# Attention scores of a hybrid retention and attention block: 288 contraction rows in two full passes and four products of 32 rows

## The chip, the cores and the metric

The kernel runs on one core of a Trainium2 chip. The metric is the device time of one execution, in microseconds (us), taken as the median of repeated runs. TensorE multiplies a stationary operand (loaded by a weight load of its own, the row "PEld") with a moving one of up to 512 columns and writes to PSUM; VectorE (DVE), ScalarE (ACT) and GpSimd (POOL) do the rest; the queue of SyncE (SP) issues most DMAs.

## What is computed

One encoder layer on 1024 tokens of width 1024: a norm, one input projection, eight heads of retention, eight heads of latent attention, one output projection with a gate. The change touches the attention scores alone. Each head has 64 columns of its own (nope) and 32 columns that carry the rotary phase (rope); the rope part of the key is one for all heads:

```python
def attend(blk):
    qn, qr = blk
    s = (jnp.einsum('bqhd,bkhd->bhqk', qn, k_nope)
         + jnp.einsum('bqhd,bkd->bhqk', qr, k_rope))
    p = jax.nn.softmax(s.astype(f32) * sm_scale, axis=-1).astype(v.dtype)
    return jnp.einsum('bhqk,bkhd->bqhd', p, v)
```

## The kernel before, in words

Every product of two f32 matrices is made of three products of a shorter type: each operand is split into a high part and the rest (low), and `mm3` (L64 to L67) adds high x high (L65), low x high (L66) and high x low (L67) into one PSUM bank. ACT writes the high part, DVE or POOL subtracts to get the low one.

After the input projection, the retention (L330 to L446, with 128-row products at L424 and products of 128 or 64 rows at L425) and the latent projections, the loop at L595 makes q and k of all heads with tokens on the partitions: `q4` and `k4` hold 96 columns per head, and L629 copies the rope columns of the key (`krp`) into each head's k. `prep` (L641) prepares one head: for each half of the tokens, four transposes (L652) put the 96 columns of q or k on the partitions, ACT writes the high part (L654, with a scale) and DVE the low part (L655); `vsplit` (L659) splits v. The first head's prep runs before the loop, with two early score blocks (`early_scores`, L670) among the value projections (L692 to L700).

The attention loop (L801) goes over 8 heads of 8 query tiles of 128 queries and, two steps behind (SKEW), over their probabilities. One step does: `scores` for tile n (L713), which is two `mm3` of 96 rows into one of two score tiles `sp` of two PSUM banks each, a maximum on DVE (L720), a scalar step (L721), the exponential on ACT (L723) and a normalisation on POOL (L724, L725); `turn` for tile n-2 (L730), which is eight transposes (L739) through three `pt` banks, casts on ACT (L741) and subtractions on DVE (L742); for every second tile `values` (L744), 24 products of 256 columns into the one `po` bank; and at set tiles (PREP_AT, for head 0 PREP_0) one part of the next head's prep. Head 7 prepares the output projection instead: pages of w_out (`w3page`, L786, in three buffers `w3h`, `w3l`) and splits of the first heads' results (`usplit`, L779). The output projection (L850) follows, one page at a time.

The instructions of each engine run in the order that the planner of the framework gives them from a model of their costs, under the data dependencies; memory that a tile gives back is waited for through semaphores.

## Time and profile before

| | us |
|---|---|
| median of 3 runs | 1059.13 (1057.57 to 1059.34) |
| the profiled execution | 1057.49 |
| its span in the trace | 1055.3 |
| TensorE busy in the span | 1018.1 (96%) |
| VectorE | 581.4 (55%) |
| ScalarE | 426.0 (40%) |
| GpSimd | 404.1 (38%) |

The profile shows one execution. Busy times of TensorE are sums over products that overlap in their pipeline, so the start of one product to the start of the next says more than the length of one. The attention loop fills the span from about 698 to 957 us.

### The profile page before, as it was taken

To read this page: it belongs to the slowest core of one execution; us is meant where nothing else is said; L and a number is where in the kernel's file an instruction comes from. 1 tells how busy PE (TensorE), PEld (TensorE's weight loads), DVE (VectorE), ACT (ScalarE), POOL (GpSimd) and SP (SyncE) were. 2 spreads that over 40 slices of the span, in tenths; PEclk is the share of its full clock that TensorE was granted. 3 is DMA by queue.
4 is the path that set the end of the run, shared out by engine and by line. 5 is a ranking of instruction groups with operands and counts; after the bars stand their busy time and mean duration, and the time that the engine had idled before them with its cause. 6 is when DMAs were issued, how large, how long until landed. Compare 5 with 4: busy or idle time off the path is not lost.

```text
span 1055.3 us, 15223 instructions
## 1 busy us (share of the span) xinstructions
PE 1018.1 (96%) x5736; PEld 888.3 (84%) x5736; DVE 581.4 (55%) x1390; ACT 426.0 (40%) x800; POOL 404.1 (38%) x311
## 2 busy tenths in 40 slices
PE   5899999999999999999999999989999999989998
PEld 4687887888888888998888889879889999878887
DVE  7996546444643534336302116777877777883342
ACT  6654213312321322124322006577767776772100
POOL 2233315213411411224633217943466555873210
PEclk8899999999999999999999999999999999998999
DMA  9721103101110212224654520100000000003522
GB/s 365 264 64 57 41 1 120 41 2 62 63 36 20 85 47 73 102 84 136 201 171 153 183 85 11 41 1 2 20 21 21 2 20 22 21 20 120 169 101 70
DMA packets 30744, 82.27 MB, mean 78 GB/s; under 512 B 3536, under 2 KB 4560, under 8 KB 30672
## 3 DMA queue, kind: packets, MB, share of 16 engines
q1 hardware_dynamic: 25920, 72.92, 20.4%
q10 hardware_dynamic: 4752, 8.39, 2.2%
q8 instruction: 45, 0.74, 0.3%
q14 instruction: 27, 0.22, 0.1%
HBM read 64.52 MB, written 16.78 MB: 77 GB/s over the span
## 4 chain that ended last, share of the span: by engine, by line
PE 82%; DVE 11%; DMA 2%; ACT 2%; issue 2%; POOL 2%; ACTq 0%; DVEq 0%; POOLq 0%
PE acc L65 13%; PE acc L66 13%; PE acc L67 13%; PE pt L739 4%; PE sp L65 4%; PE sp L66 4%; PE sp L67 4%; PE po L66 3%; PE po L67 3%; PE po L65 3%; DVE x L178 2%; DMA wa<-w_ada 2%; PE sm L425 2%; PE sm L424 1%; PE sm L65 1%
## 5 line engine op out<-in xcount | busy, mean ns | idle before, releaser
L81 POOL TENSOR_TENSOR wl<-wr,wh 128x1024 fp32r<-128x1024 f32 (+2 forms) x51 | 115.2, 2268 | 173.2 <-ACT wh L80 148.9
L65 PE MATMUL acc<-wh,hh 128*128 128x512 f32 (+2 forms) x352 | 130.8, 372 | 1.7 <-ACT hh L189 1.7
L66 PE MATMUL acc<-wl,hh 128*128 128x512 f32 (+2 forms) x352 | 130.3, 370 | 0.0
L67 PE MATMUL acc<-wh,hl 128*128 128x512 f32 (+2 forms) x352 | 126.4, 368 | 2.1 <-DVE hl L190 2.1
L725 POOL TENSOR_SCALAR pr<-pr,st 128x1024 f32<-128x1024 f32 x62 | 72.0, 1165 | 101.1 <-DVE st L724 75.5
L65 PE MATMUL acc<-hh,wh 128*128 128x512 f32 x256 | 101.0, 395 | 1.7 <-ACT v L345 1.7
L742 DVE TENSOR_TENSOR pl<-pt,ph 128x512 fp32r<-128x512 f32 x128 | 85.3, 683 | 31.2 <-ACT ph L741 31.1
L66 PE MATMUL acc<-hl,wh 128*128 128x512 f32 x256 | 100.9, 394 | 0.0
L67 PE MATMUL acc<-hh,wl 128*128 128x512 f32 x256 | 100.6, 393 | 0.0
L80 ACT CAST wh<-wr 128x1024 fp32r<-128x1024 f32 (+2 forms) x55 | 53.8, 982 | 104.1 <-PE sm L66 45.1
L741 ACT CAST ph<-pt 128x512 fp32r<-128x512 f32 x128 | 73.1, 591 | 26.6 <-PE pt L739 24.6
L720 DVE TENSOR_REDUCE st<-sp 128x1 f32<-128x1024 f32 x62 | 75.4, 1216 | 6.5 <-PE sp L67 6.4
L66 PE MATMUL po<-pl,vh 128*128 128x256 f32 x256 | 76.5, 299 | 2.1 <-DVE pl L742 2.0
L723 ACT ACTIVATE pr<-sp,st 128x1024 f32<-128x1024 f32 x62 | 69.5, 1121 | 20.8 <-DVE st L721 20.5
L65 PEld LDWEIGHTS acc<-wh,hh 128*128 128x128 f32 x352 | 67.2, 191 | 10.9 <-ACT hh L189 2.1
L67 PEld LDWEIGHTS acc<-wh,hl 128*128 128x128 f32 x352 | 66.0, 188 | 11.1 <-DVE hl L190 3.0
L66 PEld LDWEIGHTS acc<-wl,hh 128*128 128x128 f32 x352 | 67.3, 191 | 8.7
L739 PE MATMUL pt<-ident,pr 128*128 128x128 f32 x496 | 70.2, 274 | 4.0 <-DVE st L724 2.7
L65 PE MATMUL po<-ph,vh 128*128 128x256 f32 x256 | 73.3, 286 | 0.0
L67 PE MATMUL po<-ph,vl 128*128 128x256 f32 x256 | 72.8, 284 | 0.0
L360 POOL TENSOR_TENSOR rb<-t,t 128x128 f32<-128x128 f32 x32 | 14.8, 464 | 135.0 <-PE sm L370 73.4
L739 PEld LDWEIGHTS pt<-ident,pr 128*128 128x128 f32 x496 | 57.9, 141 | 8.5 <-issue 2.9
(353 smaller groups left out, 2474.2 us busy)
## 6 DMA issues: line engine op xcount, KB each, us to landing
x<-w_ada SPq DMA_DIRECT2D x16, 512.0 KB, 7.1
wr<-w_ret SPq DMA_DIRECT2D x16, 512.0 KB, 3.5
wr<-w_rg SPq DMA_DIRECT2D x8, 512.0 KB, 3.5
retD<-ro SPq DMA_DIRECT2D x16, 256.0 KB, 2.1
wr<-w_mg SPq DMA_DIRECT2D x8, 512.0 KB, 3.5
wa<-w_ada SPq DMA_DIRECT2D x8, 512.0 KB, 3.5
wr<-w_out SPq DMA_DIRECT2D x8, 512.0 KB, 4.5
wro<-retD SPq DMA_DIRECT2D x8, 512.0 KB, 3.9
```

What stands on the lines that cost most here:

```text
L65: T.matmul(out, lh, rh, start=first, stop=False, **kw)
L66: T.matmul(out, lh, rl, start=False, stop=False, **kw)
L67: T.matmul(out, ll, rh, start=False, stop=last, **kw)
L80: A.copy(out=hi, in_=raw)
L81: eng.tensor_tensor(out=lo, in0=raw, in1=hi, op=ALU.subtract)
L178: V.scalar_tensor_tensor(out=wa, in0=wa, scalar=1.0, in1=sc, op0=ALU.mult, op1=ALU.mult, accum_out=mp[:, i:i + 1])
L720: V.tensor_reduce(out=st_[:, 0:1], in_=sp, op=ALU.max, axis=AX.X)
L723: A.activation(pr, sp, AF.Exp, bias=st_[:, 1:2], scale=sc_, accum_out=st_[:, 2:3])
L725: G.tensor_scalar(out=pr, in0=pr, scalar1=st_[:, 3:4], scalar2=0.0, op0=ALU.mult, op1=ALU.add)
L739: T.transpose(tp[:, ts_(q)], pr[:, ts_(half * 4 + q)], ident)
L741: A.copy(out=ph[half][:, :, c_], in_=tv)
L742: V.tensor_tensor(out=pl[half][:, :, c_], in0=tv, in1=ph[half][:, :, c_], op=ALU.subtract)
```

## The change

The 288 rows of a score (three products of 96) are laid out anew. A first full product of 128 rows takes q1 (high nope, high rope, low rope) with k1 (high nope, high rope, high rope), a second one q2 (high nope, low nope) with k2 (low nope, high nope). What is left, high rope of q with low rope of k, has 32 rows. Two query tiles are handled together: the eight full products of both come first, then four products of 32 rows, one for each query tile and half of the keys, each on its own 32 partitions and into its own PSUM bank. `issue_after` puts the four behind the last full one on TensorE.

The rows get to their partitions by DMAs on SP's queue (`move`): seven for a half of q, one for a half of k, and 14 once for the rope part of the key. k's tile holds 64 columns per head, so its transposes have 64, and the eight copies of L629 go; `kr` keeps the rope columns. To fit in memory, the low part of q is a buffer of one half (`lo`), `sqh` has one buffer in place of two, w_out pages have two in place of three, and a page is prepared after the products that read its buffer.

```diff
@@ -589,7 +589,9 @@
     vall = p_v.tile([P, H, S], F32, name="vall", tag="vall")
     sqa = p_v.tile([P, S], F32, name="sqa", tag="sqa")
     q4 = [p_qk.tile([P, 4, H, 96], F32, name=f"q4{i}", tag=f"q4{i}") for i in range(2)]
-    k4 = [p_qk.tile([P, 4, H, 96], F32, name=f"k4{i}", tag=f"k4{i}") for i in range(2)]
+    k4 = [p_qk.tile([P, 4, H, 64], F32, name=f"k4{i}", tag=f"k4{i}") for i in range(2)]
+    kr = p_qk.tile([P, NT, 2, 16], F32, name="kr", tag="kr")
+    G.tensor_copy(out=kr, in_=krp)
     qs = [q4[t // 4][:, t % 4] for t in range(NT)]
     ks = [k4[t // 4][:, t % 4] for t in range(NT)]
     for t in range(NT):
@@ -612,7 +614,7 @@
             wh, wl = wkv[j][0]
             mm3(ps, ckh[j][:, ts_(t)], ckl[j][:, ts_(t)], wh[:, 0, 0:512], wl[:, 0, 0:512], j == 0, j == 1)
         pk = ps.rearrange("p (h d) -> p h d", h=8)
-        A.copy(out=ks[t][:, :, 0:64], in_=pk)
+        A.copy(out=ks[t], in_=pk)
         sq = p_ring.tile([P, H, 64], F32, name="sq3", tag="wr", bufs=2)
         A.activation(sq, pk, AF.Square, scale=0.125)
         V.tensor_reduce(out=ss[:, 8:16], in_=sq, op=ALU.add, axis=AX.X)
@@ -622,11 +624,10 @@
         G.tensor_tensor(out=rr, in0=ss, in1=neghalf, op=ALU.pow)
         if t == NT - 1:
             A.activation(ctile("warm", 1), rr[:, 0:1], AF.Exp, scale=0.0)
-        for x_, r0, n in ((qs[t][:, :, 0:64], 0, 64), (qs[t][:, :, 64:96], 16, 32), (ks[t][:, :, 0:64], 8, 64)):
+        for x_, r0, n in ((qs[t][:, :, 0:64], 0, 64), (qs[t][:, :, 64:96], 16, 32), (ks[t], 8, 64)):
             V.tensor_tensor(out=x_, in0=x_, in1=rr[:, r0:r0 + 8].unsqueeze(2).broadcast_to([P, 8, n]), op=ALU.mult)
         qr = qs[t][:, :, 64:96].rearrange("p h (a d) -> p h a d", a=2)
         mla_rope(qr, qr, mtab["Cq"][:, t], mtab["Sq"][:, t], 8, p_uw)
-        A.copy(out=ks[t][:, :, 64:96], in_=krp[:, t].rearrange("p a d -> p (a d)").unsqueeze(1).broadcast_to([P, 8, 32]))
     s_uw.close()
     s_cq.close()
 
@@ -635,8 +636,33 @@
     p_hd = s_hd.enter_context(tc.tile_pool(name="hd", bufs=2, side="left", reuse_waits="tile"))
     sc_ = 96.0 ** -0.5
 
-    def hd_pair(nm):
-        return (p_hd.tile([P, S], F32R, name=nm + "h", tag=nm + "h"), p_hd.tile([P, S], F32R, name=nm + "l", tag=nm + "l"))
+
+
+    k1s = [p_hd.tile([P, S], F32R, name=f"k1{z}", tag=f"k1{z}", bufs=1) for z in range(2)]
+    q3 = p_hd.tile([P, S], F32R, name="q3", tag="q3", bufs=1)
+    k3 = p_hd.tile([P, S], F32R, name="k3", tag="k3", bufs=1)
+
+    def hd_tile(nm):
+        return p_hd.tile([P, S], F32R, name=nm, tag=nm)
+
+    def q_pair():
+        return hd_tile("q1"), hd_tile("q2")
+
+    def move(dst, src):
+        SY.dma_start(out=dst.bitcast(F32), in_=src.bitcast(F32))
+
+    for half in range(2):
+        sl = slice(half * 512, half * 512 + 512)
+        tp = sm()
+        for q in range(4):
+            T.transpose(tp[0:32, ts_(q)], kr[:, half * 4 + q].rearrange("p a d -> p (a d)"), ident)
+        A.copy(out=k1s[1][0:32, sl], in_=tp[0:32])
+        V.tensor_tensor(out=k3[0:32, sl], in0=tp[0:32], in1=k1s[1][0:32, sl], op=ALU.subtract)
+        for z in range(2):
+            for r in (64, 96):
+                move(k1s[z][r:r + 32, sl], k1s[1][0:32, sl])
+        for r in (32, 64, 96):
+            move(k3[r:r + 32, sl], k3[0:32, sl])
 
     def prep(h, bank):
 
@@ -645,15 +671,29 @@
         def tr(nm, src, col, half):
             def go():
                 if half == 0:
-                    ops[nm] = hd_pair(nm)
-                hi, lo = ops[nm]
+                    ops[nm] = (k1s[h % 2], hd_tile("k2")) if nm == "k" else q_pair()
+                x1, x2 = ops[nm]
+                n = 64 if nm == "k" else 96
                 tp = bank()
                 for q in range(4):
-                    T.transpose(tp[0:96, ts_(q)], src[half * 4 + q][:, h], ident)
+                    T.transpose(tp[0:n, ts_(q)], src[half * 4 + q][:, h], ident)
                 sl = slice(half * 512, half * 512 + 512)
-                A.activation(hi[0:96, sl], tp[0:96], AF.Copy, scale=qk96[0:96, col:col + 1])
-                V.scalar_tensor_tensor(out=lo[0:96, sl], in0=tp[0:96], scalar=qk96[0:96, col:col + 1],
-                                       in1=hi[0:96, sl], op0=ALU.mult, op1=ALU.subtract)
+                A.activation(x1[0:n, sl], tp[0:n], AF.Copy, scale=qk96[0:n, col:col + 1])
+                lo = x2[:, sl] if nm == "k" else p_hd.tile([P, 512], F32R, name="lo", tag="lo", bufs=1)
+                V.scalar_tensor_tensor(out=lo[0:n], in0=tp[0:n], scalar=qk96[0:n, col:col + 1],
+                                       in1=x1[0:n, sl], op0=ALU.mult, op1=ALU.subtract)
+                if nm == "k":
+                    move(x2[64:128, sl], x1[0:64, sl])
+                else:
+                    move(x1[96:128, sl], lo[64:96])
+                    move(x2[0:64, sl], x1[0:64, sl])
+                    move(x2[64:128, sl], lo[0:64])
+                    for e in range(2):
+                        src_ = x1[64:96, sl].rearrange("p (b e n) -> p b e n", e=2, n=P)[:, :, e]
+                        c0 = 512 * (h % 2) + 256 * half
+                        for z in range(2):
+                            g = 64 * e + 32 * z
+                            move(q3[g:g + 32, c0:c0 + 256].rearrange("p (b n) -> p b n", n=P), src_)
             return go
 
         def vsplit():
@@ -664,19 +704,30 @@
             ops["v"] = (vh, vl)
         return ops, [tr("k", ks, 1, 0), tr("k", ks, 1, 1), tr("q", qs, 0, 0), tr("q", qs, 0, 1), vsplit]
 
+    def score_blocks(ops, h, blocks):
+
+        (q1, q2), (k1, k2) = ops["q"], ops["k"]
+        for i, banks in blocks:
+            for half, ps in enumerate(banks):
+                sl = slice(half * 512, half * 512 + 512)
+                T.matmul(ps, q1[:, ts_(i)], k1[:, sl], start=True, stop=False)
+                full = T.matmul(ps, q2[:, ts_(i)], k2[:, sl], start=False, stop=False)
+        with tc.issue_after(full.ins):
+            for i, banks in blocks:
+                for half, ps in enumerate(banks):
+                    r0, c0 = 64 * (i % 2) + 32 * half, 512 * (h % 2) + P * (i // 2)
+                    T.matmul(ps, q3[r0:r0 + 32, c0:c0 + P], k3[r0:r0 + 32, half * 512:half * 512 + 512],
+                             start=False, stop=True)
+
 
     early = []
 
     def early_scores(i):
-        (qh, ql), (kh, kl) = cur["q"], cur["k"]
         pr, st_ = early_pr[i], const.tile([P, 8], F32, name="ste", tag="ste", bufs=2)
-        halves = []
-        for half in range(2):
-            sl = slice(half * 512, half * 512 + 512)
-            ps = sm()
-            mm3(ps, qh[0:96, ts_(i)], ql[0:96, ts_(i)], kh[0:96, sl], kl[0:96, sl], True, True)
+        halves = [(sm(), slice(half * 512, half * 512 + 512)) for half in range(2)]
+        score_blocks(cur, 0, [(i, [ps for ps, sl in halves])])
+        for half, (ps, sl) in enumerate(halves):
             V.tensor_reduce(out=st_[:, half:half + 1], in_=ps, op=ALU.max, axis=AX.X)
-            halves.append((ps, sl))
         V.tensor_scalar(out=st_[:, 2:3], in0=st_[:, 0:1], scalar1=st_[:, 1:2], scalar2=-sc_, op0=ALU.max, op1=ALU.mult)
         for half, (ps, sl) in enumerate(halves):
             A.activation(pr[:, sl], ps, AF.Exp, bias=st_[:, 2:3], scale=sc_, accum_out=st_[:, 3 + half:4 + half])
@@ -685,7 +736,7 @@
         G.tensor_scalar(out=pr, in0=pr, scalar1=st_[:, 6:7], scalar2=0.0, op0=ALU.mult, op1=ALU.add)
         early.append(pr)
 
-    early_pr = [p_hd.tile([P, S], F32, name="epr", tag="q" + nm) for nm in "hl"]
+    early_pr = [p_hd.tile([P, S], F32, name="epr", tag="q" + nm) for nm in "12"]
     cur, todo = prep(0, sm)
     for p_ in todo[:4]:
         p_()
@@ -710,12 +761,12 @@
     def pt_bank():
         return pps.tile([P, 512], F32, name="pt", tag="pt", bufs=PT)
 
-    def scores(ops, i):
-        (qh, ql), (kh, kl) = ops["q"], ops["k"]
-        sp = pps.tile([P, S], F32, name="sp", tag="sp")
-        for half in range(2):
-            sl = slice(half * 512, half * 512 + 512)
-            mm3(sp[:, sl], qh[0:96, ts_(i)], ql[0:96, ts_(i)], kh[0:96, sl], kl[0:96, sl], True, True)
+    def scores(ops, h, i):
+        sps = [pps.tile([P, S], F32, name="sp", tag="sp") for _ in range(2)]
+        score_blocks(ops, h, [(i + z, (sp[:, 0:512], sp[:, 512:1024])) for z, sp in enumerate(sps)])
+        return [softmax(sp) for sp in sps]
+
+    def softmax(sp):
         st_ = p_at.tile([P, 4], F32, name="st", tag="st", bufs=4)
         V.tensor_reduce(out=st_[:, 0:1], in_=sp, op=ALU.max, axis=AX.X)
         V.tensor_scalar(out=st_[:, 1:2], in0=st_[:, 0:1], scalar1=-sc_, scalar2=None, op0=ALU.mult)
@@ -751,7 +802,7 @@
         if h < H - 1:
             A.copy(out=vall[:, h, sl], in_=po)
             return
-        sq = p_at.tile([P, 256], F32, name="sqh", tag="sqh", bufs=2)
+        sq = p_at.tile([P, 256], F32, name="sqh", tag="sqh", bufs=1)
         A.activation(sq, po, AF.Square)
         V.scalar_tensor_tensor(out=vall[:, h, sl], in0=po, scalar=monw[:, h:h + 1], in1=last["mg"][:, sl],
                                op0=ALU.mult, op1=ALU.mult)
@@ -764,7 +815,7 @@
         if h == 0:
             A.activation(sqa, vall[:, h], AF.Square)
         elif h < H - 1:
-            sq = p_at.tile([P, S], F32, name="sqh", tag="sqh", bufs=2)
+            sq = p_at.tile([P, S], F32, name="sqh", tag="sqh", bufs=1)
             G.tensor_tensor(out=sq, in0=vall[:, h], in1=vall[:, h], op=ALU.mult)
             G.tensor_tensor(out=sqa, in0=sqa, in1=sq, op=ALU.add)
         if h < H - 1:
@@ -787,7 +838,7 @@
         def go():
             raw = p_at.tile([P, D], F32, name="mg", tag="mg", bufs=2)
             SY.dma_start(out=raw, in_=I["w_out"][f][1])
-            hi, lo = w3h[:, f % 3], w3l[:, f % 3]
+            hi, lo = w3h[:, f % 2], w3l[:, f % 2]
             A.copy(out=hi, in_=raw)
             G.tensor_tensor(out=lo, in0=raw, in1=hi, op=ALU.subtract)
             w3[f] = (hi, lo)
@@ -806,13 +857,19 @@
             elif i == 0:
                 u3h = p_qk.tile([P, 3, S], F32R, name="u3h", tag="q40")
                 u3l = p_qk.tile([P, 3, S], F32R, name="u3l", tag="q41")
-                w3h = p_qk.tile([P, 3, D], F32R, name="w3h", tag="k40")
-                w3l = p_qk.tile([P, 3, D], F32R, name="w3l", tag="k41")
-                todo = [w3page(0), usplit(0, *hd_pair("k"), G), usplit(1, *hd_pair("q"), V), w3page(1),
+                w3h = p_qk.tile([P, 2, D], F32R, name="w3h", tag="k40")
+                w3l = p_qk.tile([P, 2, D], F32R, name="w3l", tag="k41")
+                todo = [w3page(0), usplit(0, k1s[0], hd_tile("k2"), G), usplit(1, *q_pair(), V), w3page(1),
                         usplit(2, u3h[:, 0], u3l[:, 0], V), usplit(3, u3h[:, 1], u3l[:, 1], G)]
                 last_begin()
                 uh[H - 1] = last["uh"] = (u3h[:, 2], u3l[:, 2])
-            pr = early[n] if n < len(EARLY) else scores(heads[h], i)
+            if n < len(EARLY):
+                pr = early[n]
+            elif i % 2 == 0:
+                prs = scores(heads[h], h, i)
+                pr = prs[0]
+            else:
+                pr = prs[1]
         if n >= SKEW:
             lh, li, lp = queue.pop(0)
             turn(lp, li)
@@ -829,8 +886,8 @@
 
 
     usplit(4, p_at.tile([P, S], F32R, name="vh", tag="vh", bufs=2), p_at.tile([P, S], F32R, name="vl", tag="vl", bufs=2), G)()
-    usplit(5, *hd_pair("k"), G)()
-    usplit(6, *hd_pair("q"), V)()
+    usplit(5, k1s[1], hd_tile("k2"), G)()
+    usplit(6, *q_pair(), V)()
     rb3 = sqa
 
     def branch_norm():
@@ -848,8 +905,6 @@
                 T.matmul(ps[:, ts_(q)], r3[:, t:t + 1].broadcast_to([P, P]), ident, start=True, stop=True)
             A.copy(out=rb3[:, z * 512:z * 512 + 512], in_=ps)
     for f in range(KT):
-        if f + 2 < KT:
-            w3page(f + 2)()
         hi, lo = w3[f]
         if f == KT - 1:
             out = [pt_bank()[:, 0:256] for _ in range(3)] + [pps.tile([P, 256], F32, name="po", tag="po", bufs=PO)]
@@ -864,6 +919,8 @@
             for k in range(H):
                 uh_, ul_ = uh[k]
                 mm3(y, hi[:, ts_(k)], lo[:, ts_(k)], uh_[:, sl], ul_[:, sl], k == 0, k == H - 1)
+        if f + 2 < KT:
+            w3page(f + 2)()
         if f == 0:
             branch_norm()
         for y, sl in zip(out, cols):
```

## Rows read from the trace of the kernel before

**Rows 1.** The page, parts 1 and 2: busy time; granted clock by slice.

```profile
PE 1018.1 (96%) x5736; PEld 888.3 (84%) x5736; DVE 581.4 (55%) x1390; ACT 426.0 (40%) x800; POOL 404.1 (38%) x311
...
PEclk8899999999999999999999999999999999998999
```

**Rows 2.** Windows, a head's 31 us: PE, PEld, DVE, ACT, POOL busy (count), clock, DMA.

```profile
829.00:860.00 31.00, 31.00 (x224) 28.82 (x223) 23.90 (x46) 22.27 (x42) 18.27 (x12) 1.00 0.06 18
```

**Rows 3.** Timeline of TensorE, one pair of score blocks: start us, length us.

```profile
803.18 0.48 PE L65 MATMUL sp<-kh,qh 96*128 96x512 f32 x1
803.50 0.40 PE L66 MATMUL sp<-kl,qh 96*128 96x512 f32 x1
803.73 0.40 PE L67 MATMUL sp<-kh,ql 96*128 96x512 f32 x1
...
804.65 0.60 PE L739 MATMUL pt<-ident,pr 128*128 128x128 f32 x4
...
805.45 0.48 PE L65 MATMUL sp<-kh,qh 96*128 96x512 f32 x1
...
806.93 0.28 PE L65 MATMUL po<-ph,vh 128*128 128x256 f32 x1
```

**Rows 4.** Timeline in narrow windows at 144 us: products and loads around a 64-row product.

```profile
143.96 0.28 PE L424 MATMUL sm<-v,sT 128*128 128x128 f32 x1
...
144.16 0.37 PE L425 MATMUL sm<-ST,qdT 64*128 64x128 f32 x1
144.16 0.18 PEld L425 LDWEIGHTS sm<-ST,qdT 64*128 64x128 f32 x1
...
144.37 0.27 PE L425 MATMUL sm<-ST,qdT 64*128 64x128 f32 x1
...
144.57 0.19 PEld L424 LDWEIGHTS sm<-v,sT 128*128 128x128 f32 x1
```

**Rows 5.** Timeline of the weight loads ahead of the same pair's first products.

```profile
803.15 0.19 PEld L65 LDWEIGHTS sp<-kh,qh 96*128 96x128 f32 x1
803.26 0.19 PEld L66 LDWEIGHTS sp<-kl,qh 96*128 96x128 f32 x1
```

**Rows 6.** Lines 652 and 629: count, shortest/median/longest ns, first and last start.

```profile
L652 PEld LDWEIGHTS pt<-ident,k x56: 123/126/129, 700.7 to 892.8; 128*96 128x96 f32 x56
...
L629 ACT COPY k<-krp x8: 408/418/421, 636.9 to 639.0; 128x256 f32<-128x256 f32 x8
```

**Rows 7.** Groups, 820 to 880 us: count | busy us, mean ns | idle us before, releaser.

```profile
L742 DVE TENSOR_TENSOR pl<-pt,ph 128x512 fp32r<-128x512 f32 x31 | 20.8, 684 | 9.1 <-ACT ph L741 9.1
L720 DVE TENSOR_REDUCE st<-sp 128x1 f32<-128x1024 f32 x16 | 19.4, 1215 | 0.0
...
L723 ACT ACTIVATE pr<-sp,st 128x1024 f32<-128x1024 f32 x16 | 17.9, 1120 | 5.1 <-DVE st L721 5.0
L741 ACT CAST ph<-pt 128x512 fp32r<-128x512 f32 x31 | 17.8, 589 | 6.1 <-PE pt L739 5.7
...
L663 POOL TENSOR_TENSOR vl<-vall,vh 128x1024 fp32r<-128x1024 f32 x2 | 4.8, 2396 | 0.9 <-ACT vh L662 0.9
...
L721 DVE TENSOR_SCALAR st<-st 128x1 f32<-128x1 f32 x16 | 2.3, 146 | 0.0
```

**Rows 8.** Waits of TensorE, 700 to 945 us: us in total, times, longest.

```profile
PE sp L65 <- ACT pr L723: 1.5, 3, 1.0
```

**Rows 9.** DMA issues, KB and median us to landing; SP's timeline, one issue.

```profile
pl<-xyD SPq DMA_DIRECT2D x4, 128.0 KB, 2.5
...
9.91 0.33 SPq L145 DMA_DIRECT2D wr<-w_ret  x1
```

**Rows 10.** Timelines before the loop: DVE's first q half; TensorE's early and loop scores.

```profile
689.25 0.74 DVE L655 SCALAR_TENSOR_TENSOR ql<-sm,small,qh 96x512 fp32r<-96x512 f32 x1
...
690.80 0.40 PE L65 MATMUL sm<-kh,qh 96*128 96x512 f32 x1
...
698.41 0.50 PE L65 MATMUL sp<-kh,qh 96*128 96x512 f32 x1 [1.09 <-ACT epr L682]
```

## Prediction

> **What bounds the kernel now.** I read the page's first two parts first. TensorE is busy in 96% of the span and no other engine in more than 55%, with the clock granted in full, 2.4 GHz, for nearly all of it [rows 1]; the reader is to see that only TensorE's time counts unless another engine starts to hold it up. Then I read the windows of the attention stage, one per head. In the heads in the middle TensorE has no idle time in 31 us, DVE works 23.9 us, ACT 22.3 and POOL 18.3 [rows 2]. A head is eight query tiles, so a pair of them takes about 7.8 us. Last I read TensorE's timeline of one pair [rows 3]: a 512-column product starts every 0.23 us, the first of a block of six takes 0.32 because it comes behind transposes, and from the first product to what follows a block is 1.47 us (803.18 to 804.65, 805.45 to 806.93). A pair's scores cost 2.95 us, 38% of the pair.
>
> **The pair of score blocks.** Twelve products become eight full ones and four that use 32 rows each. If the four ran in the time of one, the pair would save 0.7 us, 22 us over the 31 pairs; that is the most the change can give. Two things stand against it.
>
> The first is the change of array mode. Before, almost every product is 96 or 128 rows deep, but the retention stage has 64-row products between full ones, and they show a price [rows 4]. The second of two full 128-column products starts at 143.96. The weight load of the 64-row product begins only at 144.16, whereas within one mode loads run ahead of the product in progress. 128 columns at 2.4 GHz take 0.053 us, so about 0.147 us passes with the array emptying, then the load takes about 0.105, and the next 64-row product starts at 144.37. Going back is the same: 144.37, then a load at 144.57. Each change of mode costs about 0.19 us more than staying. Behind a 512-column product (0.213 us of columns) the step is 0.213 + 0.147 + 0.105 = 0.465 us in place of 0.23. The Trainium skill says the same in "TensorEngine Tiling (Array Packing)", Key Properties: a change of tiling mode drains TensorE. The trace agrees, with the 0.147 us above; the page states no price.
>
> The second is the spacing s at which the four products can start. No row shows 32-row products side by side. Below, s is 0 (all start together). Above, they run one after another and s is 0.23. The nearest row is the weight load: with all else free, loads of two products start 0.11 us apart (803.15 and 803.26) [rows 5]. I take s = 0.11, since each of the four brings its own load.
>
> The pair then costs 0.32 + 6 x 0.23 = 1.70 to the start of the last full product, 0.465 into the other mode, 3s, and 0.465 out: 2.63 + 3s. That is 2.96 at s = 0.11, 2.63 at 0 and 3.32 at 0.23, against 2.95. Over 31 pairs: +0.3 us, with ends -9.9 and +11.5.
>
> The two early blocks of head 0 go alone, with two narrow products each: 3 x 0.23 + 0.465 + s + 0.465 = 1.73 against 6 x 0.23 = 1.38, so +0.7 us for both.
>
> **Transposes.** The k transposes now have 64 columns of weights, not 96. Their pace is set by the product, not by the load: today's 96-column loads take 126 ns each without any stall [rows 6], so narrower gains nothing. If 64 columns are a mode of their own, each of the 16 groups pays two changes, 16 x 2 x 0.19 = 6.1 us. The nearest row is this same line at 96 columns, which pays none; I take 0 and keep 6.1 for the range. The eight new transposes of kr cost 8 x 0.11 = 0.9 us of TensorE.
>
> **What the pairing does to the other engines.** DVE's and ACT's instructions keep their number and their free size, so their time per head stays. But both score tiles of a pair end together, and the next pair needs both. From the pair's end to the next pair there are 7.8 - 2.96 = 4.85 us; the second tile is needed four products later, at 5.8. The chain is max of tile one, max of tile two (1.215 us each), the scalar step (0.15), exp of tile two (1.12): 3.7 us if nothing stands between [rows 7]. The slack of 2.1 us is three subtractions of L742 (0.684 each) or three casts of L741 (0.589). Before, TensorE waited for the exp 1.5 us in three places over the whole stage [rows 8]. Bounds: 0, and 31 x 0.65 = 20 us if four subtractions come first (3.7 + 2.7 = 6.4 against 5.8). Heads 2 to 5 have filler work, so I am near the lower end: +2 us.
>
> **The moves by DMA.** A half of q issues seven moves on SP, a half of k one: 16 per head. SP takes about 0.33 us to issue one, and 128 KB land 2.5 us after issue [rows 9]. A half of q is thus complete 7 x 0.33 + 2.5 = 4.8 us after the subtraction. In steady heads the halves of q are made in blocks 3 and 5 of the head before, 10 to 20 us ahead of use; in head 0 in blocks 5 and 6, about 8 us ahead after queueing. So nothing waits; if that cover went, a head would lose up to 4.8 us. SP spends 16 x 0.33 = 5.3 us of a head's 31; behind a waiting move stand later moves and the gate load of the next head, wanted a head later. The single lo buffer makes DVE wait for three moves of the half before (about 1 + 2.5 us); those halves are one or two blocks (3.9 or 7.8 us) apart, so this is nothing except before the first head.
>
> There it shows. The first q half's subtraction ends at 690.0, and TensorE sits idle 1.09 us at 698.41 until the early exps are done [rows 10]. With the moves the first early scores can begin at about 693 (full) and 694.8 (narrow) in place of 690.8; V projections fill in until then. DVE also waits some 2 us for lo. I take +1.5 us, bounds 0 and 4.
>
> **Edits at nothing.** The eight ACT copies of the k rope (0.418 us each) go, and nobody waited for them [rows 6], so no gain. POOL's copy of 256 elements into kr lies ahead of the loop's first normalisation. Two w_out buffers in place of three: page f+2 must wait for the products of page f, but page f+1 covers it with 48 x 0.23 = 11 us; a cast like L741's at twice its columns (1.2 us) and a subtraction like L663's (2.4 us) [rows 7] fit. If not, six pages at 3.6 us would show. The one sqh buffer serves one engine in order.
>
> **Sum.** 0.3 + 0.7 + 0.9 + 2 + 1.5 = +5.4 us. The profiled execution took 1057.5 us (span 1055.3), which gives 1062.9; the median of the three runs is 1.6 us above it, which gives 1064.5. I say 1064 us. With s between 0.08 and 0.13 (3 x 0.03 x 31 = 2.8 us down, 1.9 up) and the other terms between half and double, this case alone is 1060 to 1069.
>
> **Rivals.**
> Loads for different rows overlap. Then s is at its lower end, 0, and a pair takes 2.63: -0.32 x 31 = -9.9, with the other terms (+0.5, +0.9, +1, +1) -6.5, so 1052.6 against the median; without late tiles 1051. For it: the four products use different rows and different banks. Against it: no row shows loads less than 0.11 apart [rows 5]. The Trainium skill has a rule for it, "TensorE: Matmul & The Clock Gate", Part 3, Measured speedup vs the span model: 3.07 times for four row tiles of 512 columns. 4 x 0.23 / 3.07 = 0.30 us for the four would be s = 0.03, an estimate from that page, and the time about 1056; no trace shows it so far.
>
> The emptying is hidden as well. If the mode change cost nothing behind a long product, a pair would take 9 x 0.23 + 0.09 + 0.1 = 2.3, -0.65 x 31 = -20 us: 1041. Against it are the rows of the 64-row products.
>
> The second score tile comes free late. DVE is the place: it would be busy 24 of 31 us with two maxima back to back at each pair's end. From the point at which three subtractions stand ahead of the second maximum, each pair loses 0.3 to 0.65 us: +10 to +20, so 1073 to 1083.
>
> The change doesn't do what it says: the narrow products run one behind another, s = 0.23, +11.5 in place of 0.3: about 1076. Narrow transposes as a mode of their own add 6: about 1070.
>
> **How the numbers follow.** Even pairs with small costs (the forecast) 0.38; overlapping loads 0.29; hidden emptying 0.07; late score tiles 0.10; one behind another 0.08; narrow transposes 0.08. A measurement of this kernel can tell about 0.2% (2.1 us) from no change. Faster holds the two gains and a little of the forecast's lower edge, less the part of the overlap case that ends near zero: 0.35. Same, 1057 to 1061, holds the forecast's lower third and that part: 0.20. Slower: 0.45. Both signs are likely, so the range runs from 1048 (most of the overlap case) to 1078 (most of the slower ones); the likeliest case's own is 1060 to 1069.
>
> **What would show it.** Right: TensorE's timeline with about 0.47 us from the last full product to the second-to-next start, loads of the four 0.11 apart, heads still near 31 us, no idle in heads 2 to 5, and a later first score. Starts of the four nearly together, or loads of the four overlapping, mean the first rival; idle of TensorE before score products put down to the exp means the late tile. It would be wrong altogether if the order on TensorE put other work between the four narrow products, for each break costs two more changes of mode.

## The result

The changed kernel takes 1097.77 us (median; 1094.65 to 1098.53), the kernel before 1058.35 us on the same chip (1055.58 to 1059.34). The ratio is 1.0368 with a 95% interval of 1.0344 to 1.0392: slower by 39 us. The forecast was 1064 us with a range of 1048 to 1078, so the time lies 20 us outside the range. The profiled execution took 1098.53 us, its span is 1096.7 us.

The page of the changed kernel, parts 1 and 2 (busy time and share of the span; TensorE's busy tenths and its granted clock in 40 slices), answers to [rows 1]:

```profile
PE 1029.4 (94%) x5744; PEld 874.9 (80%) x5744; DVE 580.7 (53%) x1392; ACT 421.3 (38%) x794; POOL 401.0 (37%) x312
...
PE   5799999999999999999999999689999999879998
...
PEclk8899999999999999999999999789999999999999
```

DVE, ACT and POOL are busy as long as in [rows 1] within 5 us, TensorE 11 us longer. What is new are the 6 and 8 of TensorE in slices 26 and 27 (the start of the attention loop), the 8 and 7 in slices 35 and 36 (its end), and a lower clock at the first place.

I cut both spans at three events that each kernel has: the first score product of the loop on TensorE, ACT's copy of the first pair's values out of `po`, and the same copy 24 pairs (six heads) later. The times come from the timelines, in us; what is behind the last cut is the rest of head 6, head 7 and the output projection. Each row of this table and of the next is one profiled execution; executions of the kernel before have spans from 1054.6 to 1059.2, so differences under 2 us are not read.

| | to the first score | to the first copy | six heads | rest | span |
|---|---|---|---|---|---|
| before | 698.4 | 13.1 | 192.7 | 151.1 | 1055.3 |
| changed | 713.6 | 17.5 | 201.7 | 163.9 | 1096.7 |
| difference | +15.2 | +4.4 | +9.0 | +12.8 | +41.4 |

Windows of the middle heads (PE, PEld, DVE, ACT, POOL busy with counts, granted clock, DMA share, GB/s) answer to [rows 2]. First the changed kernel:

```profile
735.00:935.00 200.00, 186.26 (x1323) 155.66 (x1322) 143.59 (x266) 132.33 (x246) 99.23 (x68) 1.00 0.22 52
```

Then the kernel before:

```profile
735.00:935.00 200.00, 197.20 (x1390) 180.16 (x1389) 153.60 (x282) 144.22 (x260) 117.97 (x77) 1.00 0.05 17
```

TensorE had 2.8 us without work in 200 and now has 13.7, and every other engine is less busy than it was. So TensorE waits for something that is not an engine short of time. The longest waits of TensorE in the changed kernel, 720 to 1000 us (us in total, times, longest), against [rows 8]; all of them add up to 24.9 us, in the kernel before to 6.8:

```profile
PE pt L790 <- DVE pl L793: 5.7, 6, 2.2
PE sp L713 <- ACT pr L774: 5.2, 8, 2.1
PE po L65 <- ACT ph L792: 4.2, 6, 1.1
PE po L66 <- DVE pl L793: 3.3, 4, 1.3
```

Two chains hold TensorE up far longer than before: the score tile (`sp`, given back by the exponential, L774) and the split of the turned probabilities (`ph` by ACT, L792, `pl` by DVE, L793). The timeline of one pair shows how. TensorE (start, length, operation, count, and in brackets the idle time before it and what ended it):

```profile
861.68 0.39 PE L714 MATMUL sp<-k,q 128*128 128x512 f32 x1
862.00 0.51 PE L719 MATMUL sp<-k,q 32*128 32x512 f32 x4
862.44 0.39 PE L65 MATMUL po<-ph,vh 128*128 128x256 f32 x1
862.66 0.28 PE L66 MATMUL po<-pl,vh 128*128 128x256 f32 x1
...
866.03 0.64 PE L679 MATMUL pt<-ident,q 128*96 128x128 f32 x4 [0.58 <-DVE pl L793]
...
874.27 0.39 PE L65 MATMUL po<-ph,vh 128*128 128x256 f32 x1 [0.78 <-ACT ph L792]
```

DVE beside it:

```profile
862.63 2.36 DVE L771 TENSOR_REDUCE st<-sp 128x1 f32<-128x1024 f32 x2
864.90 0.27 DVE L772 TENSOR_SCALAR st<-st 128x1 f32<-128x1 f32 x2
865.28 0.69 DVE L793 TENSOR_TENSOR pl<-pt,ph 128x512 fp32r<-128x512 f32 x1
```

And ACT:

```profile
864.17 0.37 ACT L803 COPY vall<-po 128x256 f32<-128x256 f32 x1 [2.35 <-PE po L67]
864.67 0.59 ACT L792 CAST ph<-pt 128x512 fp32r<-128x512 f32 x1
865.15 1.12 ACT L774 ACTIVATE pr<-sp,st 128x1024 f32<-128x1024 f32 x1
...
866.71 1.14 ACT L774 ACTIVATE pr<-sp,st 128x1024 f32<-128x1024 f32 x1
```

The four narrow products complete both score tiles at once, so DVE takes both maxima in a row, 862.63 to 864.99. The scalar step of the first tile comes after the second maximum, at 864.90, though the first maximum was done by 863.85; the first exponential starts at 865.15, 2.5 us after the maxima began, and the second one behind it. Meanwhile ACT waits 2.35 us in its own order, for the values that it copies out of `po`, and its next cast stands behind that copy. The subtraction L793 at 865.28 follows this cast. Until it is done a `pt` bank is held, and TensorE stops before its transposes at 866.03: here the chain runs through ACT.

Elsewhere DVE's own queue holds the bank. Before the wait of 1.73 us at 973.93 (its row is shown below, with the clock), the subtraction stands directly behind two maxima and one scalar step, with no idle time on DVE:

```profile
970.87 2.35 DVE L771 TENSOR_REDUCE st<-sp 128x1 f32<-128x1024 f32 x2 [3.33 <-PE sp L719]
...
973.20 1.28 DVE L793 TENSOR_TENSOR pl<-pt,ph 128x512 fp32r<-128x512 f32 x2
```

Of the 24.9 us, 8.1 (ten waits) end in this way, with a subtraction, or the scalar step beside it, that DVE took behind a maximum without a break; 2.1 (four waits, that at 866.03 among them) end with a subtraction that had itself waited for ACT's cast; and 10.8 end with an exponential or a cast of ACT. Of the 47 maxima between 735 and 935 us in the changed kernel 17 directly follow another one; of the 50 of the kernel before none does.

### The profile page after: what moved, and what is told of

It reads as the page before. It is cut to its first block, busy times and chain, and to the rows that moved or that the text cites. A ratio compares the mean times of both kernels' runs of the same rounds, so it can differ in the third digit from the quotient of the medians.

```text
span 1096.7 us, 15543 instructions
## 1 busy us (share of the span) xinstructions
PE 1029.4 (94%) x5744; PEld 874.9 (80%) x5744; DVE 580.7 (53%) x1392; ACT 421.3 (38%) x794; POOL 401.0 (37%) x312
## 4 chain that ended last, share of the span: by engine, by line
PE 77%; DVE 11%; issue 3%; DMA 3%; ACT 3%; POOL 2%; SPq 0%; ACTq 0%; DVEq 0%; POOLq 0%
PE acc L65 13%; PE acc L66 13%; PE acc L67 13%; PE pt L790 3%; PE sp L713 3%; PE po L65 2%; PE po L66 2%; PE po L67 2%; PE sp L714 2%; DMA wa<-w_ada 2%; DVE x L178 2%; PE sp L66 2%; PE sp L65 2%; PE sp L67 2%; DVE st L771 1%
## 5 line engine op out<-in xcount | busy, mean ns | idle before, releaser
L776 POOL TENSOR_SCALAR pr<-pr,st 128x1024 f32<-128x1024 f32 x62 | 69.3, 1125 | 119.8 <-DVE st L775 80.5
L793 DVE TENSOR_TENSOR pl<-pt,ph 128x512 fp32r<-128x512 f32 x128 | 84.4, 681 | 23.8 <-ACT ph L792 23.4
L792 ACT CAST ph<-pt 128x512 fp32r<-128x512 f32 x128 | 71.2, 596 | 55.3 <-PE pt L790 54.5
L65 PE MATMUL po<-ph,vh 128*128 128x256 f32 x256 | 76.8, 300 | 4.2 <-ACT ph L792 4.2
L774 ACT ACTIVATE pr<-sp,st 128x1024 f32<-128x1024 f32 x62 | 69.4, 1123 | 16.2 <-DVE st L772 15.9
L713 PE MATMUL sp<-k,q 128*128 128x512 f32 x124 | 55.1, 444 | 11.7 <-ACT pr L774 5.2
```

The costliest lines, as they stand in the source:

```text
L65: T.matmul(out, lh, rh, start=first, stop=False, **kw)
L713: T.matmul(ps, q1[:, ts_(i)], k1[:, sl], start=True, stop=False)
L774: A.activation(pr, sp, AF.Exp, bias=st_[:, 1:2], scale=sc_, accum_out=st_[:, 2:3])
L776: G.tensor_scalar(out=pr, in0=pr, scalar1=st_[:, 3:4], scalar2=0.0, op0=ALU.mult, op1=ALU.add)
L792: A.copy(out=ph[half][:, :, c_], in_=tv)
L793: V.tensor_tensor(out=pl[half][:, :, c_], in0=tv, in1=ph[half][:, :, c_], op=ALU.subtract)
```

## The experiments

Three causes could make these differences: the two tiles of a pair finish together and crowd DVE and ACT (the pairing); the narrow products and changes of mode on TensorE; the moves by DMA, in the loop or before it. The table has the cuts of the first table for each run, as differences from the kernel before, in us.

| run | first score | first copy | six heads | rest | span |
|---|---|---|---|---|---|
| changed | +15.2 | +4.4 | +9.0 | +12.8 | +41.4 |
| pair_only | -0.9 | +3.3 | +18.1 | +14.8 | +35.4 |
| unpaired | +13.0 | +4.5 | +4.4 | -0.5 | +21.4 |
| no_narrow | +11.4 | +1.6 | -10.8 | 0.0 | +2.2 |
| short_max | +13.7 | +4.7 | -0.2 | -6.6 | +11.7 |
| before_short | -0.1 | +3.0 | -3.3 | +0.2 | -0.2 |
| narrow_mid | +12.3 | +3.1 | +5.0 | +0.9 | +21.3 |
| narrow_first | +13.6 | +1.6 | +7.2 | +10.0 | +32.5 |
| early_rope | +5.6 | +4.1 | +9.2 | +11.3 | +30.2 |
| mid_early | +3.9 | +3.0 | +4.9 | -0.6 | +11.2 |
| mid_early_pool | +6.6 | +2.9 | +4.9 | 0.0 | +14.3 |
| mid4_early | +5.0 | +1.8 | +4.5 | +7.2 | +18.5 |
| mid4_early_act | +2.8 | +1.3 | +0.9 | +7.5 | +12.6 |

**The pairing alone.** The kernel before, whose two score blocks are put together; no moves, no narrow products, the same twelve products of 96 rows.

```diff
+        for z, sp in enumerate(sps):        # two tiles, halves: kh x qh, kl x qh
...
+        with tc.issue_after(full.ins):      # then kh x ql, of both tiles
...
+        return [softmax(sp) for sp in sps]
```

> The kernel before with one thing of the change: the scores of two query tiles go together (eight products of 96 rows, then the four that are left, then both maxima and exps). No moves by DMA, no narrow products. Theory 1, the pairing itself holds TensorE up, because both score tiles are taken and given back together: the loop gets 10 to 25 us longer, 1069 to 1084. Theory 2, the loop's loss comes from the moves or from the narrow products: within 3 us of the kernel before, about 1059.

Measured: 1091.07 us, ratio 1.0298 (1.0281 to 1.0316). Pairing alone costs 32 us, against the whole change's 39, and from the first score on it costs 36 us with not one product more or less. DVE's timeline in that run:

```profile
798.97 2.36 DVE L730 TENSOR_REDUCE st<-sp 128x1 f32<-128x1024 f32 x2
801.24 0.27 DVE L731 TENSOR_SCALAR st<-st 128x1 f32<-128x1 f32 x2
801.94 0.75 DVE L655 SCALAR_TENSOR_TENSOR kl<-pt,small,kh 96x512 fp32r<-96x512 f32 x1 [0.43 <-ACT kh L654]
```

TensorE beside it waits for that subtraction:

```profile
802.74 0.42 PE L652 MATMUL pt<-ident,k 128*96 128x128 f32 x2 [0.68 <-DVE kl L655]
```

The maxima stand in a row as in the changed kernel (20 times between 735 and 935 us). The subtraction itself had waited 0.43 us for ACT (L654), and so it is with all twelve waits of TensorE for a subtraction between 760 and 900 us (9.9 us): ACT's part stands here behind its copy of `po`, for which ACT had waited 2.64 us. So the pairing is shown as the cause, and in this run's middle heads its delay reaches TensorE through ACT as well as DVE. The start is not late.

**The change without the pairing.** Each tile alone: four full products and two narrow ones.

```diff
-        sps = [pps.tile([P, S], F32, name="sp", tag="sp") for _ in range(2)]
-        score_blocks(ops, h, [(i + z, (sp[:, 0:512], sp[:, 512:1024])) for z, sp in enumerate(sps)])
-        return [softmax(sp) for sp in sps]
+        sp = pps.tile([P, S], F32, name="sp", tag="sp")
+        score_blocks(ops, h, [(i, (sp[:, 0:512], sp[:, 512:1024]))])
+        return softmax(sp)
```

> The changed kernel, but every query tile goes alone: four full products and its two narrow ones, then its softmax. Twice the changes of array mode. Theory 1, the pairing holds TensorE up: the stalls go, the mode changes cost 31 x 0.6 = 19 us more on TensorE, and the loop comes out 5 to 15 us shorter than the changed kernel's, 1083 to 1093. Theory 2, moves or mode changes are the loss: 10 to 20 us longer, 1108 to 1118.

Measured: 1078.98 us, ratio 1.0190 (1.0175 to 1.0205). The rest is back at the time of before; the heads lose 4.4 us. TensorE is full again, with four times the DMA share of before, so neither the moves nor their traffic hold the loop up:

```profile
735.00:935.00 200.00, 198.59 (x1363) 163.53 (x1361) 149.37 (x270) 141.24 (x254) 106.86 (x72) 1.00 0.23 55
```

The 4.4 us fit the changes of mode. By the starts a block on TensorE now takes 1.54 us (804.94 to 806.48) where it took 1.47 [rows 3], and the eight transposes behind it take 1.09 where eight take 1.04 without a change of mode (pair_only, at 801.02). 48 blocks of six heads by 0.12 make 5.8 us; TensorE's idle time in the window fell by 1.4:

```profile
804.94 0.48 PE L713 MATMUL sp<-k,q 128*128 128x512 f32 x1
...
806.05 0.50 PE L719 MATMUL sp<-k,q 32*128 32x512 f32 x2
806.48 1.09 PE L790 MATMUL pt<-ident,pr 128*128 128x128 f32 x8
```

**No narrow products.** The changed kernel without the four 32-row products; what high rope of q times low rope of k adds is left out.

```diff
-                full = T.matmul(ps, q2[:, ts_(i)], k2[:, sl], start=False, stop=False)
-        with tc.issue_after(full.ins):
...
+                T.matmul(ps, q2[:, ts_(i)], k2[:, sl], start=False, stop=True)
```

> The changed kernel without the four products of 32 rows (the term high rope of q times low rope of k is left out); pairing and all moves stay. If the narrow products and their mode changes cost what the trace shows (0.64 us a pair in place of 0.23 x 0): 31 x 0.6 = 19 us less if TensorE is the bound, 1079. If the loop is held up by the order of the maxima, exps and subtractions, less than half of it comes out: 1088 to 1097.

Measured: 1057.99 us, ratio 0.9995 (0.9985 to 1.0004). The tiles are still taken by twos in the code, but each is complete with its own last product, and the maxima stand apart:

```profile
801.71 1.22 DVE L765 TENSOR_REDUCE st<-sp 128x1 f32<-128x1024 f32 x1 [1.20 <-PE sp L714]
...
804.22 1.21 DVE L765 TENSOR_REDUCE st<-sp 128x1 f32<-128x1024 f32 x1
```

That is 40 us under the changed kernel and below both cases expected; the narrow products and their changes of mode are 20 us of it (31 x 0.63, worked out below). So taking the tiles by twos in the code does no harm where they end apart, and it is the common end that hurts; as TensorE has less to do here too, the run does not price that end by itself. It also shows a floor: TensorE has 0.93 us less to do per pair (2.95 - 2 x 1.01), 22 us in 24 pairs, and the six heads give 10.8, with TensorE busy 188.6 us of 200.

**Is it DVE?** The changed kernel, with each maximum taken over every 16th column and the scale of the softmax divided by 64 so that the exponentials stay in range; the output is another one.

```diff
-    sc_ = 96.0 ** -0.5
+    sc_ = 96.0 ** -0.5 / 64
...
-        V.tensor_reduce(out=st_[:, 0:1], in_=sp, op=ALU.max, axis=AX.X)
+        V.tensor_reduce(out=st_[:, 0:1], in_=sp[:, 0:1024:16], op=ALU.max, axis=AX.X)
```

> The changed kernel with maxima over every 16th column (64 in place of 1024) and a smaller softmax scale, so that nothing overflows; the output is another one. Everything else, the pairs and the taking of both tiles too, stays. If the two maxima in a row on DVE (2.4 us a pair) are what holds up the subtractions and the exps, the loop falls from 298 us to 265 to 275, 1063 to 1075. If both tiles being needed at once is enough by itself, it stays above 1085.

Measured: 1072.09 us, ratio 1.0136 (1.0113 to 1.0160). The maximum takes 0.22 us (groups, 735 to 935 us: busy, mean ns | idle before it):

```profile
L771 DVE TENSOR_REDUCE st<-sp 128x1 f32<-128x64 f32 x50 | 11.0, 221 | 9.1 <-PE sp L719 8.3
```

The windows of the same stretch:

```profile
735.00:935.00 200.00, 195.43 (x1387) 164.94 (x1386) 113.76 (x280) 141.81 (x260) 109.97 (x72) 1.00 0.24 57
```

The six heads fall by 9.2 us and the rest by 19.4; TensorE is nearly full. The same edit in the kernel before is the control:

> The kernel before with the short maxima (every 16th column) and the smaller softmax scale; the output is another one. The control of the changed kernel with short maxima (1072): theory, the loop before has no stall from DVE and TensorE is its bound, so nothing changes by more than 4 us, 1054 to 1060. If DVE was a second bound all along, it gets shorter by more than 5 us, and then the change costs more on TensorE than its trace shows.

Measured: 1058.59 us, ratio 1.0004 (0.9987 to 1.0021). Before, DVE could lose a quarter of its work (153.60 to 113.41 us in 200) and the time stayed: it was TensorE's time alone. With the pairing the same maxima are worth 26 us (1097.77 to 1072.09): an engine with room is now waited for, directly or through ACT, whose exponentials start only behind the scalar steps.

**The order within a pair.** The full products of tile 0, the four narrow ones, the full ones of tile 1, so that tile 0 is complete 1 us earlier (narrow_mid):

```diff
+        m = full(0, True)
+        with tc.issue_after(m.ins):
+            for b in range(len(blocks)):
+                m = narrow(b, b > 0)
+        if len(blocks) > 1:
+            with tc.issue_after(m.ins):
+                full(1, False)
```

And the narrow ones first (narrow_first):

```diff
+        for b in range(len(blocks)):
+            m = narrow(b, True)
+        with tc.issue_after(m.ins):
+            for b in range(len(blocks)):
+                full(b, False)
```

> The changed kernel with another order inside a pair: the four full products of the first tile, then the four narrow ones of both, then the four full ones of the second tile. The same instructions, but the first score tile is complete about 1 us before the second. Theory 1, the loop suffers because both tiles are complete at the same time (two maxima in a row on DVE, subtractions behind them): the loop falls from 298 us to 258 to 266, so 1057 to 1066. Theory 2, it suffers because both tiles are taken at the same time and so must both be free: no change, 1092 to 1100.

Measured: 1078.76 us, ratio 1.0192 (1.0172 to 1.0211). It cures the stalls (TensorE 197.76 busy in 200), but not as meant, and misses the 1057 to 1066 expected: the order puts other work between the two narrow products of tile 0 and those of tile 1. TensorE's timeline shows groups of two, each with its own two changes of mode, which is the unpaired kernel again:

```profile
802.85 0.50 PE L723 MATMUL sp<-k,q 32*128 32x512 f32 x2
...
806.20 0.50 PE L723 MATMUL sp<-k,q 32*128 32x512 f32 x2
```

> The changed kernel with the four narrow products of a pair ahead of all full ones, then the first tile's full products, then the second's. Both tiles have to be free before the pair begins, and they are complete about 1 us apart. Theory 1 (complete at the same time is what costs): close to the order with the narrow ones in the middle, 1058 to 1070. Theory 2 (taken at the same time is what costs): as the changed kernel or worse, 1095 to 1105.

Measured: 1089.51 us, ratio 1.0287 (1.0265 to 1.0309). Opening the pair with the narrow products lets the tiles end apart in part only: 13 maxima still follow one another directly, and the rest loses 10.0 us.

**The late start.** The rope part of the key is transposed and moved at the head of the q and k loop, into memory of its own; only one move per half is left for `k1` of even heads.

```diff
+    k1b = p_qk.tile([P, S], F32R, name="k11", tag="k11", bufs=1)
+    k3 = p_qk.tile([P, S], F32R, name="k3", tag="k3", bufs=1)
...
+        for r in (64, 96):
+            move(k1b[r:r + 32, sl], k1b[0:32, sl])
+        for r in (32, 64, 96):
+            move(k3[r:r + 32, sl], k3[0:32, sl])
...
+        move(k1s[0][64:128, sl], k1b[64:128, sl])
```

> The changed kernel, but the rope rows of the key lie in memory that is free before the q/k loop ends, so their ten moves go out during that loop, and k1 of the even heads gets its rows by two moves in place of eight. Theory: the late start (first loop score 15 us later than before) is SP issuing 14 rope moves at about 0.65 us ahead of the first head's: 8 us of it go away, about 1089. Rival: the late start is the first head's own q moves and the clock: within 2 us of the changed kernel, 1096 to 1098.

Measured: 1090.00 us, ratio 1.0292 (1.0271 to 1.0312). The first score comes 9.6 us earlier than in the changed kernel, at 703.98, and nothing else moves: the two losses are separate.

**Both mended.** mid_early is narrow_mid with the early rope. mid_early_pool lets POOL's queue issue the `q3` moves of the first head.

> The order with the narrow products in the middle, and the rope rows of the key moved early. If start and loop are separate costs, the 7.8 us that the early rope gave come off the kernel with the narrow ones in the middle: 1050 to 1058, at or below the kernel before. If the early start only makes the loop wait more, less than half of it comes off.

Measured: 1069.01 us, ratio 1.0100 (1.0081 to 1.0118), the best of the kernels that compute the reference with narrow products, and still slower than before. Its excess of 11.2 us in the span is, by the table, the start (3.9), the first pairs behind it (3.0) and the six heads with their changes of mode (4.9), less 0.6 in the rest.

> The kernel before this one in the list, with the eight smallest moves of the first head issued on POOL's queue. SP takes 0.55 to 0.65 us to issue one, so the first head's moves are out 5 us earlier: 2 to 5 us less if SP's issuing is still the end of the start, no change if the early exps or DVE's wait for lo is.

Measured: 1071.16 us, ratio 1.0117 (1.0100 to 1.0135): with the other queue the start came 2.7 us later, not earlier.

The last two keep the four narrow products together and still end the tiles apart: those of tile 0 stand behind those of tile 1, and the full ones of tile 1 behind both. mid4_early_act has a second `lo` buffer too, and ACT issues the first head's `q3` moves.

```diff
+        with tc.issue_after(m.ins):
+            m = narrow(1, True)
+        with tc.issue_after(m.ins):
+            m = narrow(0, False)
+        with tc.issue_after(m.ins):
+            full(1, False)
```

> As the order with the narrow products in the middle and the early rope rows, but the four narrow products of a pair are kept together: the first tile's two are queued behind the second tile's two. One group of narrow products per pair as in the changed kernel, tiles complete about 1 us apart, but both must be free at the group. In the order in the middle the planner had split the group in two, with two mode changes more per pair (0.43 us). Theory 1, complete at the same time is what cost: no stalls, 31 x 0.4 = 13 us less, 1053 to 1060. Theory 2, that both tiles must be free at once: stalls again, 1069 to 1085.

Measured: 1076.02 us, ratio 1.0168 (1.0144 to 1.0192): a miss. If only the two maxima in a row counted, this order should have beaten the kernel before. The maxima in a row are down to 7, but TensorE idles as much as in the changed kernel:

```profile
735.00:935.00 200.00, 186.77 (x1334) 161.84 (x1333) 149.65 (x270) 135.36 (x249) 107.56 (x72) 0.97 0.22 52
```

Narrow products of tile 1 that stand before its full ones need both score tiles free at one time; the longest wait of this run's loop is one of 4.7 us for the exponential that gives a tile back. With two tiles in all, a pair taken as one unit seems to be late at one end or at the other; a third tile was not tried.

> The same with two lo buffers and the eight smallest moves of the first head issued by ACT. If the rest of the late start is SP's issuing and DVE's wait for lo (2 us): 2 to 5 us less. If ACT's issuing holds up its own copies and exps instead: no change or 1 to 3 us more.

Measured: 1071.35 us, ratio 1.0124 (1.0101 to 1.0147). The first score comes 2.2 us earlier and the six heads take 3.6 us less. In the loop only the second `lo` buffer differs, so the one buffer seems to have cost something in this order; in the changed kernel's own order that was not tried.

No version beat the kernel before.

## Why the prediction was wrong

**Right: what bounds the kernel before.** TensorE alone; before_short takes a quarter of DVE's work away and gets nothing.

**Off in size: the four narrow products.** I took s = 0.11 us. The weight loads of the four start together (weight loads, same pair):

```profile
862.00 0.19 PEld L719 LDWEIGHTS sp<-k,q 32*128 32x128 f32 x4 [0.36 <-issue]
862.44 0.19 PEld L65 LDWEIGHTS po<-ph,vh 128*128 128x128 f32 x1 [0.25 <-issue]
```

So s = 0, as in the rival of overlapping loads. The last full product starts at 861.68 and its step of 0.23 ends at 861.91; the first product of the values would have started one step of 0.12 ahead of the second, 862.66, so at 862.54. The group with both its changes of mode thus takes 0.63 us. With a full block of four at 1.01 us (an entry of 0.32 and three steps of 0.23), a pair takes 2 x 1.01 + 0.63 = 2.65 us where it took 2.95: -0.30 us, some -9 us over 31 pairs, near the end of -9.9. The Trainium skill's 3.07 times ("TensorE: Matmul & The Clock Gate", Part 3, Measured speedup vs the span model) gave an estimate of 0.30 us for the four; the trace agrees, with 0.44 us from their loads to the next mode's load, less the emptying (0.147 us by [rows 4], 0.11 by the next paragraph), which is 0.29 to 0.33.

**Right: the price of a change of mode**, 0.32 us from the last full product to the narrow loads, where 0.213 + 0.147 = 0.36 was worked out, and 0.44 from these loads to the next mode's load, where it was 0.105 + 0.36 = 0.465. The emptying behind a 512-column product is then 0.32 - 0.213 = 0.11 us; it is not hidden, and that rival is out.

**The step that failed first: what the pairing does to the other engines.** I took +2 us, at most 20. The measured price is about 30 us, by three ways: pair_only loses 33 in heads and rest; short_max gives back 28.6 there to the changed kernel (25.7 by the medians of the whole time); and the changed kernel loses 21.8 there although TensorE has 9 us less to do. What failed is the chain of 3.7 us "if nothing stands between", held against a need at 5.8. In 24 pairs of the loop (743 to 941 us) the exponential of the second tile ends 6.3 us on average after the recorded end of the pair's last product. On average 2.6 us do stand between, more than the slack of 2.1: 0.4 before and between the maxima, 0.9 between the second maximum and its scalar step, both on DVE, and 1.2 between that step and the exponential, on ACT. In the kernel before the exponential ends 4.5 us after its tile's last product, in short_max the second tile's ends after 3.8. And that chain was the score tile's alone. The casts of the turned probabilities start 1.0 us after their transposes where it was 0.5; the subtractions follow their casts by 0.5 us in both kernels, so on average they are late with the casts, and behind maxima only in the places counted above. The rival of the late score tile named the place, DVE with two maxima back to back, and had 0.10; its price was bounded by the same wrong chain. My count of DVE's time (24 of 31 us) was right and says nothing on this: an engine with a quarter of its time free still answers 2.4 us late when two requests arrive at once.

I also expected filler work to cover the stalls, and looked at the middle heads [rows 2]. The loss is the largest in the rest, where the output projection's preparation is on DVE and POOL: +12.8 us there, +9.0 in six heads. There the stalls also go with a lower clock. After a wait of 1.73 us the 512-column products of the last scores start 0.43 to 0.47 us apart in place of 0.23, the 1.2 GHz level:

```profile
973.93 0.66 PE L790 MATMUL pt<-ident,pr 128*128 128x128 f32 x4 [1.73 <-DVE pl L793]
974.63 0.67 PE L713 MATMUL sp<-k,q 128*128 128x512 f32 x1
975.10 0.63 PE L714 MATMUL sp<-k,q 128*128 128x512 f32 x1
975.53 0.63 PE L713 MATMUL sp<-k,q 128*128 128x512 f32 x1
```

**The step that failed second: the start.** I took +1.5 us, bounds 0 and 4; it is +15.2. (The 4.4 us more until the first values are not all of the start's making: pair_only and before_short, with no late start, have 3.3 and 3.0 there.) I had priced the first head's seven moves and put no term for the 14 moves of the key's rope. The lines that transpose and cast it (count, shortest/median/longest, first and last start):

```profile
L658 PE MATMUL sm<-ident,kr x8: 272/273/275, 642.7 to 658.5; 128*32 128x128 f32 x8
```

and the cast that follows, with what ended its wait:

```profile
L659 ACT CAST k<-sm x2: 572/573/574, 689.2 to 689.7; 32x512 fp32r<-32x512 f32 x2
its engine sat idle before it (us, times) until:
  POOL q L494: 1.3, 1
```

The transposes are done by 658.5, the casts come at 689.2: `k1` lies in memory that the q and k loop still uses, and the last user is POOL (L494). So all 14 moves start at that moment, with the two of k's halves, ahead of the q moves in the one queue (SP's timeline):

```profile
689.81 10.88 SPq L652 DMA_DIRECT2D k<-k  x16
700.78 0.55 SPq L652 DMA_DIRECT2D q<-lo  x1
702.66 2.67 SPq L652 DMA_DIRECT2D q<-q  x4
```

An issue takes 10.88 / 16 = 0.68 us, not the 0.33 of a load from memory [rows 9]; landing, 1.9 to 2.3 us after issue, is as expected. DVE waits 10.3 us for the single `lo`, where I had some 2:

```profile
704.53 0.75 DVE L683 SCALAR_TENSOR_TENSOR lo<-sm,small,q 96x512 fp32r<-96x512 f32 x1 [10.29 <-DMA q<-lo]
```

and TensorE twice; then it starts the loop at the 1.2 GHz level (0.43 us between products):

```profile
702.83 1.62 PE L713 MATMUL sm<-k,q 128*128 128x512 f32 x3 [6.06 <-issue]
...
713.63 0.80 PE L713 MATMUL sp<-k,q 128*128 128x512 f32 x1 [4.91 <-ACT epr L733]
714.22 0.63 PE L714 MATMUL sp<-k,q 128*128 128x512 f32 x1
714.65 0.63 PE L713 MATMUL sp<-k,q 128*128 128x512 f32 x1
```

The windows give a granted clock of 0.76 for the stretch around the loop's start and of 0.83 for that at its end:

```profile
704.00:735.00 31.00, 24.64 (x129) 17.36 (x128) 19.42 (x36) 13.60 (x28) 7.04 (x6) 0.76 0.23 62
...
971.00:981.00 10.00, 8.22 (x46) 6.68 (x45) 7.38 (x14) 6.28 (x12) 6.54 (x5) 0.83 0.17 52
```

Of the +15.2 us early_rope gives back 9.6: memory and queue of the rope moves. What is left, 5.6, is a little over the bound of 4.

**Right: what I costed at nothing.** Transposes of 64 columns run at 273 ns each, in overlapped groups, with no step for a mode (groups, 735 to 935 us):

```profile
L679 PE MATMUL pt<-ident,k 128*64 128x128 f32 x48 | 7.2, 273 | 0.0
```

The output projection with two buffers of w_out costs nothing: with the tiles apart the rest is as long as before (unpaired -0.5). The moves of the later heads are hidden in steady state (unpaired, TensorE 198.59 of 200 busy); in the changed kernel one wait of 1.4 us, at 739.79, is put down to one.

**Still open.** In short_max the pairs cost TensorE 0.30 us less each, 7 us in six heads, but the six heads are only 0.2 us shorter than before. Part of it is that the order there splits groups (32 narrow groups for 24 pairs' worth of products between 735 and 925 us, each with its changes of mode), part is 4.6 us of idle time in 200; I did not separate the two. Nor was the order on DVE and ACT varied by itself: with the first tile's scalar step directly behind its maximum, or ACT's copy of `po` behind the exponentials, part of the pairing's price might go. That is a rival to the length of the maxima as the thing to mend, and no run tests it.

## What to carry to other kernels

Before two pieces of work are merged so that they end together, list what the engine that takes them over has queued behind, and count the delay of that work and of the engine behind it, not the busy share: here a pairing that put two maxima of 1.2 us in a row cost some 30 us, on an engine that was busy 55%. A gain on the bounding engine of 0.30 us per pair did not pay for two units that were apart by half a period and now arrive at once. And for every moved or early step ask which memory it is given: a tile that takes over another stage's memory starts when that stage's last reader is done, whatever its own inputs are.

## What the runs showed of the hardware

Weight loads of four products on different rows start together (four in 0.19 us), where two loads on the same rows stand 0.11 us apart [rows 5]; and a group of two narrow products takes as long as one of four (806.05 to 806.48, and 862.00 to 862.44), so the price is that of the group, nearly all of it the change of mode.

A move from one set of partitions to another takes SP's queue 0.54 to 0.68 us to issue, up to twice the 0.33 us of a load in [rows 9], and with the eight `q3` moves of the first head on POOL's queue the first score came 2.7 us later (705.03 and 702.31; the medians are 2.2 us apart).
